# Experts taken in an order that is listed on the chip, and computed in 64-row parts first

## The chip, the cores and the metric

The kernel runs on one NeuronCore of a Trainium2 chip. The metric is device time in microseconds (us) of one execution, the median of several runs. The kernel before takes 1252.5 us (three runs: 1251.7, 1252.5, 1255.65).

The engines are named as in the profile: PE (TensorE, matrix multiplication; PEld are its weight loads), DVE (VectorE), ACT (ScalarE), POOL (GpSimd) and SP (SyncE, which here only issues DMAs). Each engine works through its own queue in order and waits for the others by semaphores.

## The reference, cut to what matters

One layer of a streaming encoder on 512 tokens of 1024 features. A token mixer (projection, gated MLP, gated delta rule, output projection) comes first; then a layer norm; then a hierarchical mixture of experts, which is what the change touches; then a last layer norm.

```python
def _hier_moe(x, w_rg, b_rg, w_re, b_re, w1, w3, w2):
    pg = softmax(xt @ w_rg + b_rg); grp = argmax(pg)            # top 1 of 4 groups
    le = (xt @ w_re + b_re) of that group                        # 8 experts in a group
    top_v, top_i = lax.top_k(le, MOE_TOPK)                       # top 2 of the 8
    gate = p_grp * softmax(top_v)
    eid = grp * MOE_EXPERTS_PER_GROUP + top_i                    # 32 experts
    ...
    hb = silu(xb @ w1[e]) * (xb @ w3[e]);  y = hb @ w2[e]        # 1024 -> 512 -> 1024
    ...
    out = sum over the two experts of gate * y
```

The 1024 pairs (512 tokens, two experts each) are spread unevenly. The reference's routing of the inputs that the kernel gets, experts 0 to 31 in four groups of eight:

```
all tokens       1   0   2   2   1   2   1   1
                57  55  40  18  94  83  37 130
                34  22  82 104  15  18 126  19
                 0  11   8   5  26  15  13   2
first 256        0   0   1   2   1   1   1   0
                29  30  16  11  40  36  16  62
                18  12  43  54   5  12  65   5
                 0   7   5   4  17   8  11   0
```

Two experts (1 and 24) get no token; five (0, 1, 7, 24, 31) get none from the first 256 tokens. Eleven get more than 32, six more than 64, three more than 96, none more than 160.

## The kernel before, in words

The program has a front (normalisation, projections, gated MLP, delta rule, merge), which the change leaves alone. Then come three stages.

**Output projection, first norm, router** (`out_ln1`, `Router`). The 512 tokens are four tiles t of 128. For each tile PE does 48 matmuls (`po`, helper line L416), transposes the rows (`ph`, L433) and multiplies them with the router's weights (`lps`, L987). DVE makes the tile's logits (`lg`, L991), and `Router.tile` finds the two experts of each token (`ek`, L1078), marks them (`mk`, `M`), counts with small matmuls how many earlier tokens chose the same expert (`cps`, L1083), and scatters the token's number into its expert's list (`sps`, L1097). After the last tile `sort` writes the lists of token rows, `idx`: up to 160 (NB) per expert. The instruction order of this stage is set by a scheduler from its own estimates.

**The experts** (`Experts.run`), written by hand in order. A block b is one expert: position b in the list `blocks`, which goes through j = 0 to 7 and within it through the groups, so experts 0, 8, 16, 24, 1, 9, 17, 25, 2 and so on. An expert's weights are six chunks of 1 MB: four of w1 and w3 together (chunks 0 to 3), two of w2 (4, 5). SP loads them in the order in which PE uses them: chunks 0 to 3 of block b, then 4 and 5 of block b-1. There are 18 buffers (`raws`), used in turn; a load waits until the matmuls that read its buffer's chunk of 18 places earlier are done, and until the load eight places earlier has landed. The first 18 loads are unconditional (13 go out early, the last five, `late`, once the router's memory is free); each later one has a condition on its expert's count and moves nothing for an empty expert.

In step b the program does: gather the rows of block b+2 from DRAM (`fetch`, POOL; 64 rows, and 96 more if the count is over 64); `up` of block b on PE (x times w1 and w3); silu and product (`gate`: ACT, DVE); `turn_x` of block b+1 (PE transposes, DVE scales the result into `x`); `down` of block b-1 on PE (h times w2); `turn` of block b (PE transposes h, ACT copies); `store_y` of block b-1 (DVE and ACT copy out of PSUM, POOL issues the stores to `y_dram`). `up` and `down` work in parts (`parts`): rows 0 to 31 always (the small part: 32-column weights, four column groups of PE side by side), rows 32 to 95 if the count is over 32, rows 96 to 159 if it is over 96 (the large parts: 64 columns, two groups). Up to five copies of a block for counts over 160 follow in a loop; here it runs zero times.

**The end** (`finish_rows`, `finish`): SP loads the normalised rows and the gain and bias rows behind the last weights, ACT and DVE scale them, then, after the loop's barrier, POOL gathers each token's two expert rows from `y_dram`, and DVE, ACT and POOL do the last norm.

In the profile L1371 is `up`'s matmul, L1399 `down`'s, L1350 and L1356 the transposes of `turn_x`, L1385 and L1387 those of `turn`, L1378 and L1379 `gate`, L1407 and L1410 the copies of `store_y`, L1416 its stores, L1331 the gathers, L396 and L398 the weight loads without and with a condition, L1248 and L1283 the clearing before the first block. Line numbers of the changed kernel differ: there L417 is `po`, L1127 `cps`, L1141 `sps`, L397 and L399 the loads, L1484 and L1489 the stores.

## Time and profile before

| | us |
|---|---|
| median of three runs | 1252.5 |
| the profiled execution | 1258.0 |
| its span, first to last instruction | 1256.0 |
| before the first expert's matmul | 703.0 |
| from there to the end of the last | 495.4 |
| after it | 57.6 |

One execution was profiled; its span is 2 us shorter than its time, and its time is 5.5 us over the median. Times of instructions are counted from the span's start. In the span cut into 40 slices (31.4 us each) a digit is the busy share in tenths; "GB/s" is what the DMA engines moved. TensorE's mean granted clock over the span is 0.937. A matmul of 32-bit floats shows as two records. Of the DMAs, 192 weight loads are issued, and those whose condition is false move nothing.

### The profile page before, as it was taken

The page shows a single profiled execution, that of the slowest core. Times are in us where ns is not written, and L with a number is a line of the kernel's source. Part 1 is how long each engine was busy: PE and PEld are TensorE (multiplying, and loading weights), DVE is VectorE, ACT ScalarE, POOL GpSimd, SP SyncE. Part 2 cuts the span into 40 slices and gives each one's busy share as a digit, 9 for nine tenths or more (in the row PEclk, how much of TensorE's full clock was granted, in tenths as well). Part 3 has the DMA queues.
Part 4 walks back from the last instruction along what each step waited for, and adds up shares of the span by engine and source line. Part 5 has one row for each costly group of instructions (what it writes and reads, how often), then busy time and mean ns, then how long its engine had stood idle before and what let it go on. Part 6 is the DMA issues. An engine that isn't in the chain of part 4 may idle for free. (4 is left out here: it accounts for less than half of the span.)

```text
span 1256.0 us, 20781 instructions
## 1 busy us (share of the span) xinstructions
PE 1080.5 (86%) x7740; PEld 708.2 (56%) x7740; DVE 616.5 (49%) x1266; ACT 440.0 (35%) x902; POOL 185.6 (15%) x374
## 2 busy tenths in 40 slices
PE   4999999999999999999999688898798786799910
PEld 2888788867777777667887344444344333234400
DVE  7566444567667777744754434423123132222256
ACT  6333355444545455435331222323122222122221
POOL 1000100311321133300000111112011111011034
PEclk9999999999999999999999799999799798799965
DMA  4422533899112122015674749999999999999953
GB/s 171 151 84 68 164 90 121 288 339 356 56 63 68 35 67 68 24 45 189 218 284 165 267 161 397 408 398 403 407 400 406 400 414 410 385 418 386 405 188 129
DMA packets 77182, 298.15 MB, mean 237 GB/s; under 512 B 9360, under 2 KB 34208, under 8 KB 53248
## 3 DMA queue, kind: packets, MB, share of 16 engines
q1 hardware_dynamic: 66960, 274.22, 57.9%
q0 software_dynamic: 7504, 17.20, 4.1%
q10 hardware_dynamic: 2592, 4.99, 1.1%
q8 instruction: 86, 1.41, 0.5%
q14 instruction: 40, 0.33, 0.1%
HBM read 277.36 MB, written 50.35 MB: 261 GB/s over the span
## 5 line engine op out<-in xcount | busy, mean ns | idle before, releaser
L1371 PE MATMUL u<-raw,x 128*32 128x256 f32 (+1 forms) x2496 | 231.5, 440 | 30.1 <-DMA raw<-in_w 27.7
L213 PE MATMUL psi<-hTh,lo 128*128 128x512 f32 x448 | 183.7, 412 | 1.6 <-DVE lo L213 1.6
L213 PE MATMUL psi<-hTh,hi 128*128 128x512 f32 x448 | 184.0, 414 | 0.9 <-ACT hi L213 0.5
L213 PE MATMUL psi<-hTl,hi 128*128 128x512 f32 x448 | 183.6, 412 | 0.0
L1371 PEld LDWEIGHTS u<-raw,x 128*32 128x32 f32 (+1 forms) x2496 | 96.8, 119 | 150.2 <-issue 69.1
L1379 DVE TENSOR_TENSOR h<-h,u 128x640 f32<-128x640 f32 x32 | 26.3, 821 | 307.1 <-ACT h L1378 307.1
L213 DVE TENSOR_TENSOR lo<-raw,hi 128x1024 fp32r<-128x1024 f32 x74 | 91.4, 1236 | 78.5 <-ACT hi L213 77.5
L213 ACT CAST hi<-raw 128x1024 fp32r<-128x1024 f32 x74 | 77.5, 1047 | 120.2 <-PE psi L213 103.2
L1399 PE MATMUL yz<-raw,hT 128*32 128x256 f32 x1024 | 80.6, 457 | 21.3 <-DMA raw<-in_w 10.3
L213 PEld LDWEIGHTS psi<-hTh,lo 128*128 128x128 f32 x448 | 84.8, 189 | 21.4 <-issue 3.9
L213 PEld LDWEIGHTS psi<-hTh,hi 128*128 128x128 f32 x448 | 85.0, 190 | 20.5 <-issue 2.8
L213 PEld LDWEIGHTS psi<-hTl,hi 128*128 128x128 f32 x448 | 84.8, 190 | 17.3 <-issue 1.6
L1378 ACT ACTIVATE h<-u 128x640 f32<-128x640 f32 x32 | 22.5, 703 | 178.7 <-PEq L1319 130.6
L1410 ACT COPY ylarge<-y 64x512 f32<-64x512 f32 x128 | 74.3, 580 | 9.1 <-DMA y_dram<-ylarge 7.6
L1407 DVE COPY ysmall<-yz 32x256 f32<-32x256 f32 x128 | 53.5, 418 | 44.5 <-PE yz L1399 36.5
L1388 ACT COPY hT<-t 128x128 f32<-128x128 f32 x32 | 8.5, 265 | 190.7 <-PE t L1385 190.7
L1399 PEld LDWEIGHTS yz<-raw,hT 128*32 128x32 f32 x1024 | 39.0, 126 | 49.3 <-issue 25.9
L1416 POOL DMA_DIRECT2D y_dram<-ysmall x32 | 15.9, 497 | 304.7 <-DVE ysmall L1407 267.5
L213 DVE SCALAR_TENSOR_TENSOR acc<-xp,cols,acc 128x512 f32<-128x512 f32 x72 | 54.6, 759 | 4.7 <-ACT acc L213 3.5
L1399 PE MATMUL y<-raw,hT 128*64 128x512 f32 x224 | 51.0, 602 | 0.0
L1350 PE MATMUL t<-ident,mh 64*128 64x64 f32 x256 | 24.5, 240 | 23.3 <-PEq L1319 14.8
L1350 PEld LDWEIGHTS t<-ident,mh 64*128 64x128 f32 x256 | 20.4, 151 | 42.8 <-issue 39.8
(403 smaller groups left out, 1764.9 us busy)
## 6 DMA issues: line engine op xcount, KB each, us to landing
raw<-in_w SPq DMA_DIRECT2D x192, 1024.0 KB, 20.7
raw<-in_wt SPq DMA_DIRECT2D x73, 512.0 KB, 3.8
y_dram<-zero SPq DMA_DIRECT2D x48, 512.0 KB, 6.5
y_dram<-ylarge POOLq DMA_DIRECT2D x128, 128.0 KB
raw<-in_wv SPq DMA_DIRECT2D x8, 512.0 KB, 7.6
raw<-in_wo SPq DMA_DIRECT2D x4, 1024.0 KB, 8.2
y_dram<-ysmall POOLq DMA_DIRECT2D x32, 128.0 KB
vt<-in_x SPq DMA_DIRECT2D x4, 512.0 KB
```

The costliest lines, as they stand in the source:

```text
L213: op._ins = getattr(getattr(self.nc, op.attr), op.name)(*map(real, op.args), **{k: real(x) for k, x in op.kw.items()})
L1350: nc.tensor.transpose(self.t[0][:, k * NA:k * NA + NA], r[0][:, k * 128:k * 128 + 128], ident[0:NA, 0:NA])
L1371: self.nc.tensor.matmul(self.u[q * r:(q + 1) * r, NP if p is None else p, 0:c], x[:, k, r0:r0 + r], self.raw[b, k // 2][:, o:o + c], start ...
L1378: self.nc.scalar.activation(out=h, in_=u[:, :, 0], func=AF.Silu)
L1379: self.nc.vector.tensor_mul(out=h, in0=h, in1=u[:, :, 1])
L1388: self.nc.scalar.copy(out=x[:, n], in_=self.t[1][:, 0:128])
L1399: self.nc.tensor.matmul(y[q * r:(q + 1) * r, 0:c], t[:, i, j * r:(j + 1) * r], self.raw[b, 4 + k // 2][:, o:o + c], start=k == 0, stop=k == 3)
L1407: nc.vector.tensor_copy(out=small[:, q], in_=self.y0[q * 32:(q + 1) * 32, 0:256])
L1410: nc.scalar.copy(out=large[:, q, p], in_=self.y[p][q * 64:(q + 1) * 64])
L1416: nc.gpsimd.dma_start(out=dst.rearrange("r (q n) -> r q n", q=src.shape[1]), in_=src, cond=c > 32 * j)
```

## The change

**The order of the experts.** `Router.order` runs between tiles 1 and 2. It counts, for the first 256 tokens, how many chose each expert, flags the experts with at least one (the first three of the old order, 0, 8 and 16, are always flagged), and writes a list `ord` of 32 places: the flagged experts in the old order, but the last four of them at the very end, and the unflagged ones just ahead of these four. With these inputs the list is 0, 8, 16, 9, 17, 25, 2, 10, 18, 26, 3, 11, 19, 27, 4, 12, 20, 28, 5, 13, 21, 29, 6, 14, then 24, 1, 7, 31, then 22, 30, 15, 23. Marking, counting and scattering (`place`) work with places in this list instead of experts, and so have to follow it: those of tiles 0 and 1 both come after `order`. Blocks 0 to 2 load their weights by fixed addresses; from block 3 on SP loads the expert's number (`ordi`) into a register and the weights from an address made with it.

**The parts.** Large parts of 64 rows come first: rows 0 to 63 if the count is over 32, rows 64 to 127 if it is over 96. What is left over, if anything, is the small part of 32 rows, which starts at row 0, 64 or 128. `units` makes three numbers per expert: the count (at most 160), the rest d behind the large parts, and the small part's first row r0. The small part, always done before, is done only if d is over 0; so a count of 0, of 33 to 64 or of 97 to 128 has none. Its 32 columns stand in a tile of their own, `xs`, which DVE fills first, and for counts over 64 fills again from the row r0.

**The stores.** The small part is stored at a row made with r0, if d is over 0. A large part is stored in two DMAs of 64 rows by 512 columns, where it was two of 32 rows by 1024. ACT's four copies of 64 partitions are two of 128.

**Clearing.** PSUM is cleared by six ACT copies with scale 0 instead of DVE, the unused columns of `x` by POOL.

The diff, without the changes of the overflow loop and of constants:

```diff
@@ -38,6 +38,7 @@
+NPRE = 3
...
@@ -990,6 +991,11 @@
                 router.tile(t)
+                if t == 1:
+                    router.order()
+                    router.place(0)
+                if t:
+                    router.place(t)
...
+
+    def order(self):
+
+
+        nc, W, cst, v, g = self.nc, self.W, self.cst, self.nc.vector, self.nc.gpsimd
+        for t in range(2):
+            q = W.tile([128, 2, E], BF, name="oq")
+            v.tensor_tensor(out=q, in0=bc(cst["iota"][:, 0:E], 2, 1), in1=bc(self.ek[:, :, t], E, 2), op=OP.is_equal)
+            for k in range(2):
+                nc.tensor.matmul(self.cps[:, NT], cst["ones_bf"], q[:, k], start=t + k == 0, stop=t + k == 2)
+        f = W.tile([128, E], F32, name="of_")
+        v.tensor_scalar(f.rearrange("p (j g) -> p j g", g=4), self.cps[:, NT].rearrange("p (g j) -> p j g", g=4),
+                        0.0, None, op0=OP.is_gt)
+        v.memset(f[:, 0:NPRE], 1.0)
+        r = W.tile([128, E], F32, name="or_")
+        v.tensor_tensor_scan(r, cst["ones"][:, 0:E], f, 0.0, OP.mult, OP.add)
+        b = W.tile([128, 2], F32, name="ob_")
+        v.tensor_scalar(b[:, 0:1], r[:, E - 1:E], -4.0, float(NPRE), op0=OP.add, op1=OP.max)
+        v.tensor_scalar(b[:, 1:2], r[:, E - 1:E], -1.0, float(E), op0=OP.mult, op1=OP.add)
...
+        eq = W.tile([128, E, E], F32, name="oeq")
+        v.tensor_tensor(out=eq, in0=bc(p0, E, 1), in1=bc(cst["iota"][:, 0:E], E, 2), op=OP.is_equal)
+        g.tensor_tensor(out=eq, in0=eq, in1=bc(cst["seq"], E, 1), op=OP.mult)
+        v.tensor_reduce(out=self.ord, in_=eq, axis=AX.X, op=OP.add)
+        v.tensor_copy(out=self.ordi, in_=self.ord)
+
+    def place(self, t):
+
+        nc, W, cst, v = self.nc, self.W, self.cst, self.nc.vector
         mk = self.mk[:, :, t]
-        v.tensor_tensor(out=mk, in0=bc(cst["iota"][:, 0:E], 2, 1), in1=bc(ef, E, 2), op=OP.is_equal)
+        v.tensor_tensor(out=mk, in0=bc(self.ord, 2, 1), in1=bc(self.ek[:, :, t], E, 2), op=OP.is_equal)
         v.tensor_tensor(out=self.M[:, t], in0=mk[:, 0], in1=mk[:, 1], op=OP.add)
...
+    def units(self, W, n, out):
+
+
+        v, w = self.nc.vector, n.shape[1]
+        a = W.tile([128, 3, w], F32, name="un%d" % w)
+        v.tensor_scalar(a[:, 1], n, 32.0, 64.0, op0=OP.is_gt, op1=OP.mult)
+        v.tensor_scalar(a[:, 2], n, 96.0, 64.0, op0=OP.is_gt, op1=OP.mult)
+        v.tensor_tensor(out=a[:, 2], in0=a[:, 2], in1=a[:, 1], op=OP.add)
+        v.tensor_scalar(a[:, 0], n, float(NB), None, op0=OP.min)
+        v.tensor_tensor(out=a[:, 1], in0=a[:, 0], in1=a[:, 2], op=OP.subtract)
+        v.tensor_copy(out=out, in_=a)
+
...
     def clear(self):
 
-        for t in [self.u[:, 0:NP]] + self.y + [x[:, :, NA:96] for x in self.x]:
-            self.nc.vector.memset(t, 0.0)
+        for t in [self.u[:, NP, 0:256]] + [self.u[:, p] for p in range(NP)] + [self.y0[:, 0:256]] + self.y:
+            n = t.shape[1] // 128
+            self.nc.scalar.activation(out=t.rearrange("p (a n) -> p a n", a=n), in_=bc(self.cst["ident"], n, 1),
+                                      func=AF.Copy, scale=0.0)
 
...
         load(len(kk.raws) - late, True)
+        if clear:
+            for x in self.x:
+                nc.gpsimd.memset(x[:, :, NA:96], 0.0)
         for b in range(min(2, nb)):
             self.fetch(b, 0)
+        if clear:
+            clear()
         next(more, None)
         for b in range(min(2, nb)):
             self.fetch(b, 1)
         if clear:
-            clear()
 
...
     def parts(self, b, f):
 
-        n = self.n(b)
-        f(b, None)
+        n, d = self.n(b), self.n(b, ET.PE, 1)
+        with self.tc.If(d > 0):
+            f(b, None)
         with ExitStack() as st:
             for p in range(NP):
                 st.enter_context(self.tc.If(n > 32 + 64 * p))
...
-        affine(slice(0, NA), ((self.t[0], 0, KD),))
+        affine(xs, slice(0, 32), ((self.t[0], 0, KD),))
+        affine(x, slice(0, NA), ((self.t[0], 0, KD),))
...
         with self.tc.If(self.n(b, ET.DVE) > NA):
-            affine(slice(NA, NB), zs)
+            affine(x, slice(NA, NB), zs)
+            v.tensor_copy(out=xs, in_=x[:, :, ds(self.n(b, ET.DVE, 2), 32)])
 
     def place(self, p):
 
-        return (4, 0, 32) if p is None else (2, 32 + 64 * p, 64)
+        return (4, 0, 32) if p is None else (2, 64 * p, 64)
...
-        x, (n, r0, r) = self.s[b]["x"], self.place(p)
+        x, (n, r0, r) = self.xs[b % 2] if p is None else self.s[b]["x"], self.place(p)
...
@@ -1402,22 +1475,19 @@
     def store_y(self, b):
         nc, row = self.nc, self.blocks[b][0]
         small = self.yp.tile([32, 4, 256], F32, name="ysmall")
-        large = self.yp.tile([64, 2, NP, 512], F32, name="ylarge")
+        large = self.yp.tile([128, NP, 512], F32, name="ylarge")
         for q in range(4):
             nc.vector.tensor_copy(out=small[:, q], in_=self.y0[q * 32:(q + 1) * 32, 0:256])
         for p in range(NP):
+            nc.scalar.copy(out=large[:, p], in_=self.y[p])
+        n, d, r0 = (self.n(b, ET.Pool, i) for i in range(3))
+        nc.gpsimd.dma_start(out=self.y_dram[ds(row + r0, 32), :], in_=small.rearrange("r q n -> r (q n)"), cond=d > 0)
+        for p in range(NP):
+            r = row + 64 * p
+            dst = self.y_dram[r:r + 64, :] if isinstance(row, int) else self.y_dram[ds(r, 64), :]
             for q in range(2):
-                nc.scalar.copy(out=large[:, q, p], in_=self.y[p][q * 64:(q + 1) * 64])
-        c = self.n(b, ET.Pool)
-
-        def store(j, src):
-            r = row + j * 32
-            dst = self.y_dram[r:r + 32, :] if isinstance(row, int) else self.y_dram[ds(r, 32), :]
-            nc.gpsimd.dma_start(out=dst.rearrange("r (q n) -> r q n", q=src.shape[1]), in_=src, cond=c > 32 * j)
-
-        store(0, small)
-        for j in range(2 * NP):
-            store(1 + j, large[j % 2 * 32:j % 2 * 32 + 32, :, j // 2])
+                nc.gpsimd.dma_start(out=dst[:, q * 512:(q + 1) * 512], in_=large[q * 64:(q + 1) * 64, p],
+                                    cond=n > 32 + 64 * p)
...
@@ -1574,9 +1644,9 @@
 
 
 
-    blocks = [(e * NB, static(e), r.idx[0:NA, 0, e:e + 1], r.idx[0:NB - NA, 1, e:e + 1], r.cnti[0:1, e:e + 1],
-               True)
-              for i, e in enumerate(g * 8 + j for j in range(8) for g in range(4))]
+    blocks = [(e * NB, static(e % 4 * 8 + e // 4) if e < NPRE else dynamic(r.ordi[0:1, e:e + 1]), r.idx[0:NA, 0, e:e + 1],
+               r.idx[0:NB - NA, 1, e:e + 1], [r.cnti[0:1, i, e:e + 1] for i in range(3)], e >= NPRE)
+              for e in range(E)]
     with tc.manual_schedule():
         ex.run(blocks, rest, ex.clear)
         for _ in rest:
...
```

In the next three places the rows are those of one engine's queue, in order; x4 is a row four times over.

PE in `out_ln1`, around the last matmuls of tile 2 and the first of tile 3 (`po`; its weight tiles are hi and lo, `mh` and `ml` the tokens). Before:

```order
L416 MATMUL po<-lo_4855,mh 128x512 x4
L416 MATMUL po<-hi_4839,mh 128x512
L416 MATMUL po<-hi_4839,ml 128x512
L416 MATMUL po<-hi_4839,mh 128x512
L416 MATMUL po<-hi_4839,ml 128x512
L433 MATMUL ph<-ident,h1s_4469 128x128 [waits DVE_49]
```

With the change:

```order
L417 MATMUL po<-lo_4857,mh 128x512 x3
L1127 LDWEIGHTS ustrict
L1127 MATMUL cps<-M,ustrict 128x32 [waits DVE_49]
L417 MATMUL po<-lo_4857,mh 128x512
L417 MATMUL po<-hi_4841,mh 128x512
L1127 LDWEIGHTS ones_bf
L1127 MATMUL cps<-M,ones_bf 128x32 [waits DVE_49]
```

The counting matmuls of tiles 0 and 1, which stood in their own tiles, now stand before tile 2's last matmul and wait there for DVE's `M`, which waits for the list.

POOL in `store_y` of one block (DMASW_n are the lanes on which its DMAs report; ISA rows set the condition). Before:

```order
L1416 DMA y_dram<-ysmall 32x1024 [waits DMASW5_49,DVE_49]
L1416 ISA
L1416 DMA y_dram<-ylarge 64x1x512 [waits DMASW6_49,Activation_49]
```

With the change:

```order
L1379 TENSOR_LOAD cnti x2
L1484 ISA
L1484 DMA y_dram<-ysmall 32x1024 [waits DMASW7_49,DVE_49]
L1489 ISA
L1489 DMA y_dram<-ylarge 64x512 [waits DMASW7_49,DMASW0_49,Activation_49]
```

POOL reads d and r0 into registers at this place, and the first large store now also waits for the lane of the small store ahead of it (DMASW7), that is, until that has landed.

SP at the first expert's loads (DMAHW_n: lanes of SP's DMAs), from the change:

```order
L397 DMA raw_5396<-in_w 128x2048 [waits DMAHW0_49,DVE_49,PE_49]
L1639 TENSOR_LOAD ordi [waits DVE_49]
L397 ISA
L397 DMA raw_5397<-in_w 128x2048 [waits DMAHW1_49,DVE_49,PE_49]
```

The load of an expert's number stands ahead of its first chunk; before, the row ahead of a DMA without condition was the DMA of the chunk before it.

More of the change, by code (lines that the diff above doesn't have):

```diff
@@ L1078, in tile @@
         v.tensor_copy(out=ef, in_=e8[:, 0:2])
+    def order(self):
[14 more added lines that the diff above has]
+        v.tensor_scalar(b[:, 1:2], r[:, E - 1:E], -1.0, float(E), op0=OP.mult, op1=OP.add)
+        p0 = W.tile([128, E], F32, name="op0")
+        v.scalar_tensor_tensor(out=p0, in0=cst["iota"][:, 0:E], scalar=b[:, 0:1], in1=r, op0=OP.add, op1=OP.subtract)
+        p1 = W.tile([128, E], F32, name="op1")
+        v.tensor_scalar(p1, r, b[:, 0:1], b[:, 1:2], op0=OP.is_gt, op1=OP.mult)
+        v.scalar_tensor_tensor(out=p1, in0=r, scalar=-1.0, in1=p1, op0=OP.add, op1=OP.add)
+        v.tensor_tensor(out=p1, in0=p1, in1=p0, op=OP.subtract)
+        v.tensor_tensor(out=p1, in0=p1, in1=f, op=OP.mult)
+        v.tensor_tensor(out=p0, in0=p0, in1=p1, op=OP.add)
+        eq = W.tile([128, E, E], F32, name="oeq")
[3 more added lines that the diff above has]
+        v.tensor_copy(out=self.ordi, in_=self.ord)
@@ L1119, in rest @@
         yield
-        v.tensor_copy(out=self.cnti, in_=cnt)
+        self.units(R, cnt, self.cnti)
         gs = R.tile([128, NT, 4], F32, name="gs")
@@ L1165, in rest @@
         ot = R.tile([128, 7, NX * E], F32, name="ot")
-        for j, src in enumerate((cst["eidx"], stb[:, 0].rearrange("p b e -> p (b e)"),
+        ei = R.tile([128, NX, E], F32, name="ei")
+        v.tensor_copy(out=ei, in_=bc(self.ord, NX, 1))
+        for j, src in enumerate((ei.rearrange("p b e -> p (b e)"), stb[:, 0].rearrange("p b e -> p (b e)"),
                                  stb[:, 1].rearrange("p b e -> p (b e)"))):
@@ L1170, in rest @@
             v.tensor_reduce(out=self.of[:, j], in_=ot, axis=AX.X, op=OP.add)
-            if j < 2:
-                v.tensor_copy(out=self.oi[:, j], in_=self.of[:, j])
+            if j == 0:
+                v.tensor_copy(out=self.oi[:, 0], in_=self.of[:, 0])
             yield
+        self.units(R, self.of[:, 1], self.oi[:, 1:4])
+        yield
         dst = R.tile([128, NT, E], F32, name="dst")
@@ L1240, in __init__ @@
         self.x = [xt.tile([128, KD, NB], F32, name="x%d" % i) for i in range(2)]
+        self.xs = [xt.tile([128, KD, 32], F32, name="xs%d" % i) for i in range(2)]
         self.hp = self.ec(self.tile_pool(name="ehp", bufs=1))
@@ L1306, in run, with n @@
             next(more, None)
-    def n(self, b, e=ET.PE):
+    def n(self, b, e=ET.PE, i=0):
         s = self.s[b]
-        if ("n", e) not in s:
-            s["n", e] = self.nc.values_load(self.blocks[b][4], engines=(e,), min_val=-T, max_val=T,
-                                            skip_runtime_bounds_check_because="counts of tokens")
-        return s["n", e]
+        if ("n", e, i) not in s:
+            lo, hi = ((0, NB), (-64, 32), (0, 128))[i]
+            s["n", e, i] = self.nc.values_load(self.blocks[b][4][i], engines=(e,), min_val=lo, max_val=hi,
+                                               skip_runtime_bounds_check_because="counts of tokens")
+        return s["n", e, i]
     def parts(self, b, f):
-        n = self.n(b)
-        f(b, None)
+        n, d = self.n(b), self.n(b, ET.PE, 1)
+        with self.tc.If(d > 0):
+            f(b, None)
         with ExitStack() as st:
```

28 lines of the change are left out of this document (16 added, 12 removed).

## The prediction

> **What bounds the kernel now.** I read the page first, then the slices, stage windows, SP's timeline and PE's timeline at the experts' end. PE looks like the bound (86% busy), but the slices say otherwise for the second half.
>
> ```profile
> PE   4999999999999999999999688898798786799910
> DMA  4422533899112122015674749999999999999953
> GB/s 171 151 84 68 164 90 121 288 339 356 56 63 68 35 67 68 24 45 189 218 284 165 267 161 397 408 398 403 407 400 406 400 414 410 385 418 386 405 188 129
> ```
>
> From slice 25 to 38 the DMA engines are full at about 400 GB/s. The windows give the edges of that stretch.
>
> ```profile
> 700.00:722.00 22.00, 17.64 (x173) 8.82 (x175) 5.83 (x24) 1.55 (x3) 1.99 (x3) 0.79 0.93 351
> 722.00:741.00 19.00, 17.25 (x170) 7.80 (x170) 6.72 (x13) 4.47 (x8) 1.67 (x6) 1.00 0.08 17
> 741.00:1195.00 454.00, 379.05 (x3839) 177.24 (x3832) 129.90 (x248) 109.68 (x203) 61.21 (x178) 0.91 1.01 402
> 1195.00:1256.00 61.00, 2.43 (x37) 1.38 (x35) 37.39 (x49) 12.35 (x16) 22.44 (x25) 0.55 0.42 151
> ```
>
> The last two columns are DMA share and GB/s. For 454 us the DMA is the bound (1.01); just before, for 19 us, it does nearly nothing (0.08) while 182 MB (454 us at 402 GB/s) are still to come. SP's rows say why.
>
> ```profile
> 700.84 2.91 SPq L396 DMA_DIRECT2D raw<-in_w  x5
> 708.07 20.03 SPq L398 DMA_DIRECT2D raw<-in_w  x10
> 739.12 2.49 SPq L398 DMA_DIRECT2D raw<-in_w  x4
> raw<-in_w SPq DMA_DIRECT2D x192, 1024.0 KB, 20.7
> q1 hardware_dynamic: 66960, 274.22, 57.9%
> q0 software_dynamic: 7504, 17.20, 4.1%
> ```
>
> Blocks 3 and 4 are experts 24 and 1, which are empty. Of the ten loads issued from 708.07, only block 2's two w2 chunks move anything: the other eight places in the list are the empty experts' (chunks 2 and 3 of block 3, all of block 4, 4 and 5 of block 3). The next real load needs `up` of block 2 to end, and goes out at 739.12. So the empty experts use up buffers when PE has none to give back. Ten of the 192 loads move nothing; two of the empty experts' twelve are among the 18 unconditional ones.
>
> **The change, term by term**, against the profiled span of 1256.0. A chunk is 1.049 MB, so at 402 GB/s 2.61 us. Landing 20.7 us after issue means that eight share the engines.
>
> *The gap.* With the new list, what follows `up` of block 0 is block 3's and 2's chunks and then block 4's, all real: four at about 708, six more after `up` of block 1. Backlog at 708 is still the five late loads (13 us), so the gap goes: 0.92 x 19 = **-17.5**.
>
> *Two chunks fewer.* The empty experts now stand at places 24 and 25, where all twelve loads have a condition: 2 x 2.61 = **-5.2**.
>
> *The list.* It lengthens the router's chain.
>
> ```profile
> 665.24 0.17 DVE L1078 CAST ek<-e 128x2 f32<-128x2 uint32 x1
> 665.94 0.18 PE L1083 MATMUL cps<-M,ustrict 128*128 128x32 bf16 x1 [0.35 <-DVE M L1081]
> 674.74 0.39 PE L416 MATMUL po<-hi,mh 128*128 128x512 f32 x1
> 727.38 0.86 DVE L1155 TENSOR_TENSOR ov<-inc,iota 128x672 f32<-128x672 f32 x1 [0.22 <-DVEq L1357]
> 754.98 0.85 DVE L1170 TENSOR_REDUCE of<-ot 128x7 f32<-128x672 f32 x1
> L1033 POOL TENSOR_TENSOR raw<-raw,raw 128x1024 f32<-128x1024 f32 x3 | 7.0, 2337 | 6.7 <-DVE ve L369 5.8 <-DVE nm L373 0.9
> 689.83 0.69 DVE L977 SCALAR_TENSOR_TENSOR h1s<-po,h1s 128x512 f32<-128x512 f32 x1 [5.96 <-PE po L416]
> 690.55 0.69 DVE L979 BATCH_NORM_STATS2 st<-h1s 128x6 f32<-128x512 f32 x1
> ```
>
> From `ek` of tile 1 (665.4): some 13 small DVE steps at about 0.23 apart (3.0), tile 2's addition and statistics that stand between them (1.4), the comparison and the sum over 1024 elements (0.86 and 0.85 for 672, so 1.3 each), POOL's product (2.34), the marks (1.0): 10.3, so `M` at about 675.7. PE reaches the waiting matmul, one before tile 3's at 674.74, at about 673.9 (six matmuls moved away ahead of it): a stall of 1.8. The ones moved here add 1.2 more, and all that follows on PE and DVE, up to the last tile's list, is later by **3** (bounds 0 and 6: the stall vanishes, or doubles). The late loads wait for DVE's clearing:
>
> ```profile
> 698.16 0.91 DVE L1248 MEMSET u<- 128x1024 f32 x1 [0.21 <-issue]
> 699.13 1.03 DVE L1248 MEMSET y<- 128x512 f32 x2
> 700.20 0.55 DVE L1248 MEMSET x<- 128x256 f32 x2
> ```
>
> These 2.5 go to ACT and POOL, and six small steps (`units`, 1.3) come: 1.2 back. The stream starts **+1.8** later. ACT's six copies end before `up` of block 0 needs them, since its x must first be gathered; if not, PE starts 1 or 2 us later, which the stream doesn't feel.
>
> *A hole at the empties.* Places 24 and 25 use twelve of 18 buffers. After the chunks of block 23 and 22 that are eight in flight, the next real one (block 26) needs `up` of block 23 done. Eight that share the engines have some 4.5 chunks of work left together; when the fourth lands, 1.25 (3.3 us). `up` ends 1.7 after it, and a load needs some 2 us before it moves anything (estimate from the 256 KB stores' 2.0 to landing, below). I take **+2** (0 to 6).
>
> ```profile
> h_dram<-h1s ACTq DMA_DIRECT2D x8, 256.0 KB, 2.0
> L1416 POOL DMA_DIRECT2D y_dram<-ysmall x32 | 15.9, 497 | 304.7 <-DVE ysmall L1407 267.5 <-DVE stb L1163 21.1 <-DMA y_dram<-ysmall 16.1
> ```
>
> *Stores in pieces of 2 KB.* The rows stored stay the same. The 14 large parts' 3.67 MB cost at q0's 51.5 us per 17.2 MB 11.0. By bytes halving the pieces is free, by packets it adds 11. q1's mean packet is 4.1 KB at 2.65 us per MB, q0's 2.3 KB at 2.99: nearly half the size, 13% dearer. So **+2**.
>
> *PE.* Nine small parts go (37 to 57, 104, 126 tokens and the empties), some 5.6 us of PE each, and each `parts` gets a branch and each block a register load, below 0.5. In a stretch where PE waits for weights neither shows.
>
> *The tail.* Where PE follows the last weights, the order of the last experts counts.
>
> ```profile
> 1152.09 18.29 PE L1371 MATMUL u<-raw,x 128*32 128x256 f32 x128
> 1178.11 0.68 PE L1350 MATMUL t<-ident,mh 64*128 64x64 f32 x8 [0.34 <-PEq L1319]
> 1179.09 1.93 PE L1399 MATMUL yz<-raw,hT 128*32 128x256 f32 x32 [0.30 <-PEq L1353]
> 1180.95 7.09 PE L1399 MATMUL y<-raw,hT 128*64 128x512 f32 x32
> 1188.66 3.66 PE L1371 MATMUL u<-raw,x 128*32 128x256 f32 x64
> 1196.46 1.93 PE L1399 MATMUL yz<-raw,hT 128*32 128x256 f32 x32 [0.96 <-ACT hT L1389]
> ```
>
> Before, expert 15 (130 tokens: 18.3 us of `up`, 9.0 of `down`) is third from last, and 16 chunks follow its w13 (42 us), in which PE catches up: it ends at 1198.4, 3.4 after the stream (1195). Now expert 15 is the last but one, and ten chunks follow (26.1). From its last w13 chunk on PE does: rest of the small part 0.9, both large parts and branches 14.2, `turn_x` 1.6, `down` of expert 30 2.3, `turn` 0.7, `up` of 23 4.0, `turn_x` place 1.6, `down` of 15 9.3, `turn` and ACT's copies 2.0, `down` of 23 1.9: 38.5. So PE ends 12.4 after the stream: **+9** (5 to 14).
>
> [...]
>
> *The end.* ACT's L1410 copies halve, but the stores of 130 tokens now precede the last ones by one block, and the first of them waits for the small one: I take it over as it was, 57.6.
>
> Sum: -17.5 - 5.2 + 1.8 + 2 + 2 + 9 = -7.9, a span of 1248.1; the median stands 3.5 under the span: **1244.5**.
>
> **The rivals.**
>
> *PE does not lag at the end.* Then the tail's 9, and perhaps the hole and the pieces (4), fall away: 1231.5 to 1235.5. For it: the stream was the bound up to 1195 and PE 0.83 busy. Against: the chain above is made of quoted matmuls. 0.2.
>
> *The gain is given back in the stores.* If a 2 KB piece costs like a 4 KB one, +9, and if the large store's wait for the small one holds ACT's queue in the tail (the next silu is behind its copies), some 2 more: 1253.5 to 1256. For it: smaller packets are dearer by the byte. Against: q0's are dearer by 13% only, at nearly half q1's size. 0.15.
>
> *SP becomes the bound: slower.* 162 moving loads get an address from a register, which no row here shows. Now four loads take SP 2.49, 0.62 each. From 2.61 per load on SP sets the pace and every 0.1 us costs 16: at 2.8, 31 us, so 1276. Against: the loads with a condition use a register too and are no dearer than those without (2.91 for five). 0.12.
>
> That the list misses the empties is excluded by the table of the first 256 tokens: experts 1 and 24 are unflagged.
>
> **How the numbers follow.** Forecast 0.53. Less than 0.3% (3.8 us) can't be told from no change. Of the forecast's own spread (1238 to 1251, by the start, the hole and the tail) 0.48 lies below 1248.7; with the first rival that is 0.68 faster. The rest, 0.05 of the forecast and most of the stores, is 0.19 same; SP and the stores' far end 0.13 slower. Range: all bounds good and half the tail, 1232; hole, start and tail bad, 1257.
>
> **What would show it.** DMA share near 1 from 701 on without the 19 us at 0.08; last weight at about 1178; expert 15's `up` starting some 26 us before that and PE ending 12 after; an idle DMA of a few us around 1065; the last tile's `h1s` about 3 later than 689.83 (quoted). It is wrong if SP's loads come more than 2.61 apart with fewer than eight in flight, if chunks take over 2.7 in the full stretch, or if PE ends within 5 us of the last landing.

## The result, and the profile after

The changed kernel takes 1245.92 us (median of five runs, 1242.91 to 1248.74), the kernel before 1255.65 in the same comparison: a ratio of 0.9926, with a 95% interval of 0.9897 to 0.9955. Measured a second time, beside the first experiments, it was 0.9902 (0.9880 to 0.9925). The forecast was 1244.5 in a range of 1232 to 1257, so it holds. Whether its steps hold is another matter, and the experiments found some that don't.

The slices of the changed kernel, as they were shown of the one before (31.0 us each):

```profile
DMA  4422433899222121113673799999999999999942
GB/s 172 156 83 69 156 99 105 284 347 358 76 69 53 50 69 52 35 52 135 244 303 106 285 371 406 396 410 401 417 392 415 397 412 400 381 384 386 387 121 109
```

Its windows: the two that held the old gap, the full stretch, the place of the empty experts, and the tail from expert 22 on (columns: length, busy time of the five engines, granted clock, DMA share, GB/s).

```profile
700.00:722.00 22.00, 12.21 (x101) 6.43 (x103) 6.19 (x17) 2.08 (x5) 1.86 (x2) 0.70 1.00 361
722.00:741.00 19.00, 15.88 (x108) 6.85 (x106) 8.43 (x17) 3.23 (x6) 0.73 (x5) 1.00 0.93 372
741.00:1176.00 435.00, 334.26 (x3079) 154.41 (x3077) 153.91 (x318) 73.89 (x145) 61.68 (x177) 0.89 1.01 401
1060.00:1068.00 8.00, 2.76 (x29) 1.74 (x25) 4.85 (x10) 2.53 (x5) 0.66 (x4) 0.81 0.75 288
1109.40:1184.00 74.60, 69.11 (x564) 29.66 (x564) 19.44 (x39) 10.33 (x21) 8.23 (x25) 0.96 0.93 366
```

The 19 us that stood at a DMA share of 0.08 are now at 0.93. At the empties there is a hole of 8 x 0.25 = 2 us. The rate in the full stretch is the same, 401 GB/s. Now the end of the stream and the tail, on SP and PE; the last of SP's `in_rows` loads goes out as the last weight lands, eight loads behind it, so the end of its group marks the landing. Before:

```profile
1187.45 8.31 SPq L1009 DMA_DIRECT2D raw<-in_rows  x4
```

With the change:

```profile
1161.76 7.84 SPq L1015 DMA_DIRECT2D raw<-in_rows  x4
1146.27 3.66 PE L1444 MATMUL u<-raw,xs 128*32 128x256 f32 x64
1149.86 13.96 PE L1444 MATMUL u<-raw,x 128*64 128x512 f32 x64
1174.33 7.09 PE L1472 MATMUL y<-raw,hT 128*64 128x512 f32 x32
1182.08 1.93 PE L1472 MATMUL yz<-raw,hT 128*32 128x256 f32 x32
```

The last weight lands at 1169.6 instead of 1195.8, and PE, with expert 15's `up` and `down` in the tail, ends at 1184.0, 14.4 behind it; before it was 2.6. So 12 of the 26 us by which the last weight lands earlier are given back in the tail, about as forecast.

All kernels of this study in the same stages, each from its one profiled run. "h1s" is the start of DVE's last `h1s`, which ends the router's input; "late" the first of the five late loads, "landed" the last weight. The time up to h1s differs by a few us between profiled runs of one kernel (687.5 and 689.3 for the changed one), so it is left out here.

| kernel | h1s to late | late to landed | to PE's end | to the end | ratio to before |
|---|---|---|---|---|---|
| before | 11.0 | 494.9 | 2.6 | 57.6 | 1 |
| changed | 9.2 | 472.9 | 14.4 | 57.2 | 0.9926 |
| changed, again | 9.2 | 476.1 | 13.5 | 57.6 | 0.9902 |
| old list | 9.2 | 499.8 | 5.8 | 61.1 | 1.0055 |
| order alone | 11.0 | 470.3 | 21.2 | 58.7 | 0.9968 |
| empties early | 9.2 | 495.5 | 8.1 | 59.3 | 1.0056 |
| small part always | 9.2 | 485.1 | 20.6 | 57.7 | 1.0047 |
| clearing on DVE | 13.2 | 469.9 | 13.5 | 57.8 | 0.9927 |
| list fixed | 9.6 | 475.0 | 12.8 | 57.3 | 0.9892 |
| reversed | 9.2 | 477.0 | 5.4 | 60.0 | 0.9908 |
| light last | 9.2 | 478.8 | 0.7 | 61.9 | 0.9876 |
| light last, large stores first | 9.2 | 477.4 | 2.2 | 55.1 | 0.9866 |
| rows early | 9.2 | 476.7 | 12.9 | 57.9 | 0.9907 |
| order alone, light last | 11.1 | 471.2 | 1.8 | 55.7 | 0.9794 |

The ratios' intervals are about 0.002 to either side (0.0014 for the order alone, 0.003 for the first measurement of the changed kernel). One thousandth is 1.26 us.

### The profile page after: what moved, and what is told of

Its sections match the earlier page's. It is cut to its first block, busy times and chain, and to the rows that moved or that the text cites. A ratio compares the mean times of both kernels' runs of the same rounds, so it can differ in the third digit from the quotient of the medians.

```text
span 1241.2 us, 19396 instructions
## 1 busy us (share of the span) xinstructions
PE 1031.0 (83%) x6880; PEld 681.0 (55%) x6880; DVE 645.1 (52%) x1358; ACT 403.3 (32%) x844; POOL 192.0 (15%) x377
## 3 DMA queue, kind: packets, MB, share of 16 engines
q1 hardware_dynamic: 66672, 272.13, 57.9%
q0 software_dynamic: 7504, 17.20, 4.3%
## 5 line engine op out<-in xcount | busy, mean ns | idle before, releaser
L1444 PE MATMUL u<-raw,xs 128*32 128x256 f32 x1472 | 100.1, 421 | 31.0 <-DMA raw<-in_w 27.8
L1444 PE MATMUL u<-raw,x 128*64 128x512 f32 x448 | 105.0, 623 | 6.6 <-PEq L1386 2.7
L214 PEld LDWEIGHTS psi<-hTh,lo 128*128 128x128 f32 x448 | 84.5, 189 | 21.2 <-issue 3.9
L1444 PEld LDWEIGHTS u<-raw,xs 128*32 128x32 f32 x1472 | 48.4, 118 | 74.6 <-DMA raw<-in_w 35.1
L1444 PEld LDWEIGHTS u<-raw,x 128*64 128x64 f32 x448 | 34.4, 144 | 71.6 <-issue 59.2
L1472 PE MATMUL y<-raw,hT 128*64 128x512 f32 x224 | 60.2, 692 | 15.4 <-PEq L1386 12.7
L1472 PE MATMUL yz<-raw,hT 128*32 128x256 f32 x736 | 52.3, 420 | 12.6 <-PEq L1425 6.1
L1489 POOL DMA_DIRECT2D y_dram<-ylarge x128 | 19.5, 154 | 195.4 <-DMA y_dram<-ysmall 115.3
L1421 PE MATMUL t<-ident,mh 64*128 64x64 f32 x256 | 23.7, 238 | 27.2 <-PEq L1388 15.9
L1472 PEld LDWEIGHTS y<-raw,hT 128*64 128x64 f32 x224 | 19.4, 158 | 48.9 <-issue 48.6
```

Of the source, the lines that this page charges most:

```text
L214: op._ins = getattr(getattr(self.nc, op.attr), op.name)(*map(real, op.args), **{k: real(x) for k, x in op.kw.items()})
L1421: nc.tensor.transpose(self.t[0][:, k * NA:k * NA + NA], r[0][:, k * 128:k * 128 + 128], ident[0:NA, 0:NA])
L1444: self.nc.tensor.matmul(self.u[q * r:(q + 1) * r, NP if p is None else p, 0:c], x[:, k, r0:r0 + r], self.raw[b, k // 2][:, o:o + c], start ...
L1472: self.nc.tensor.matmul(y[q * r:(q + 1) * r, 0:c], t[:, i, j * r:(j + 1) * r], self.raw[b, 4 + k // 2][:, o:o + c], start=k == 0, stop=k == 3)
L1489: nc.gpsimd.dma_start(out=dst[:, q * 512:(q + 1) * 512], in_=large[q * 64:(q + 1) * 64, p], cond=n > 32 + 64 * p)
```

## The experiments

The theory is the prediction's: the loads are the bound, the list takes the gap out of them, and the heavy expert near the end gives half of it back. The chief rival: it is the time that the 64-row parts save PE.

**The changed kernel again, and with the old list.** The second is made by flagging every expert, so that the list, computed as before, comes out as the old order.

```diff
-        v.memset(f[:, 0:NPRE], 1.0)
+        v.memset(f, 1.0)
```

> The changed kernel once more, as the yardstick of this call. Both theories: the ratio to the kernel before is 0.993 as measured (0.990 to 0.9955).

> Every expert is flagged, so that the computed list is the old order; parts, stores, clearing and the list's own cost stay. Theory (the order is what counts, the loads are the bound): against the changed kernel the gap comes back (DMA idle 18.6 us of the first 40 before, 3.3 now: +15), two more chunks are loaded (2.1 MB at 2.5 us: +5), and PE ends 3 us after the last landing as it did before, not 14.4 (-11.5): +9 in all, ratio to before about 1.000. Rival (the gain comes from the parts: PE busy 334 of 435 us in the full stretch against 379 of 454): the gain stays, ratio 0.993 or less.

Measured: 0.9902 and 1.0055. The rival is out: with the parts but without the order the kernel is slower than before. But the distance is 19 us where the theory gave 9. Some 6 of these ten stand behind the last landing: PE ends 5.8 behind it, not 3, and the end is 61.1, not 57.6. The others stand in the gap. The first 45 us from the first late load on, old list:

```profile
698.60:743.60 45.00, 29.52 (x202) 13.89 (x202) 13.31 (x34) 8.54 (x16) 4.39 (x9) 0.74 0.49 176
```

Before:

```profile
700.80:745.80 45.00, 39.26 (x377) 17.96 (x375) 15.60 (x39) 6.03 (x11) 4.07 (x9) 0.91 0.60 224
```

A DMA share of 0.49 against 0.60: the gap is 23 us with the changed parts, clearing and stores, and was 18. PE has done less by then (29.5 us of work against 39.3). POOL's first gather and PE's first matmuls say what is late. Before:

```profile
697.75 1.12 POOL L1331 DMA_INDIRECT mh<-h_dram,idx  x1 [5.36 <-DVE idx L1103]
700.37 1.09 PE L1350 MATMUL t<-ident,mh 64*128 64x64 f32 x8 [2.85 <-DMA mh<-h_dram,idx]
702.97 4.94 PE L1371 MATMUL u<-raw,x 128*32 128x256 f32 x64 [1.51 <-DVE x L1347]
```

With the change:

```profile
687.49 0.69 DVE L978 SCALAR_TENSOR_TENSOR h1s<-po,h1s 128x512 f32<-128x512 f32 x1 [5.95 <-PE po L417]
696.41 1.13 POOL L1400 DMA_INDIRECT mh<-h_dram,idx  x1 [0.85 <-DVE cnti L1257]
696.71 3.14 SPq L397 DMA_DIRECT2D raw<-in_w  x5
703.38 1.09 PE L1421 MATMUL t<-ident,mh 64*128 64x64 f32 x8 [8.19 <-DMA mh<-h_dram,idx]
707.02 5.06 PE L1444 MATMUL u<-raw,xs 128*32 128x256 f32 x64 [2.56 <-DVEq L1429]
```

From the gather's start to PE's first transpose it was 2.6 us and is now 7.0 (+4.4): the five late loads (5 MB) go out 0.3 us behind it, where they went out 3.1 behind it before. The gather starts 1.0 later against h1s, with the `units` ahead of it (its wait names `cnti`), and from the transposes to `up` it is 1.0 more, with four DVE operations for `x` in place of two. So PE's first `up` starts 19.5 us after h1s; it was 13.1. Loads wait for PE's `up` there, so the stream feels it.

**The order alone.** The kernel before with the changed kernel's list in its program text.

```diff
-              for i, e in enumerate(g * 8 + j for j in range(8) for g in range(4))]
+              for i, e in enumerate((0, 8, 16, 9, 17, 25, 2, 10, 18, 26, 3, 11, 19, 27, 4, 12, 20, 28, 5, 13, 21,
+                                     29, 6, 14, 24, 1, 7, 31, 22, 30, 15, 23))]
```

> The kernel before with nothing but the order: its list of experts, in the program text, is the one that the changed kernel makes on the chip (0, 8, 16, 9, 17, 25, ..., 24, 1, 7, 31, 22, 30, 15, 23). Parts, stores, clearing, marks and fixed addresses as before. Theory (the order brings the stream's gain, the 64-row parts matter only where PE does not wait, which is at the front and from expert 22 on): loads start 11 after h1s, PE 13; the gap goes (-15 to -18) and two chunks (-5); but expert 22 (126 tokens) has its small part again in the tail, so PE ends 18 to 21 after the last landing (+15 to +18), as with the small part always done: -4 to -8 in all, ratio 0.994 to 0.997. Rival (the parts are worth nothing in this order, and the order is all): 0.990 or less.

Measured: 0.9968, as the theory said. Stage by stage the stream is 24.6 shorter (20 to 23 were expected), and PE ends 21.2 behind it. Its first 45 us, then those of the changed kernel's two profiles:

```profile
699.20:744.20 45.00, 39.23 (x376) 17.93 (x375) 15.60 (x39) 6.04 (x11) 4.08 (x9) 0.91 1.00 387
696.70:741.70 45.00, 28.80 (x210) 13.60 (x212) 15.79 (x38) 8.57 (x16) 4.39 (x9) 0.82 0.94 355
698.50:743.50 45.00, 29.38 (x202) 13.80 (x202) 13.76 (x34) 8.56 (x16) 4.21 (x5) 0.75 0.88 335
```

With the order alone the DMAs are never idle there. In the changed kernel the share was 0.94 and 0.88, so its own front loses 3 to 5 us that the order had won. What its parts win is in the tail, 21.2 to 14: expert 22 (126 tokens) has no small part any more.

**The empties early.** The place of the unflagged experts is one constant of the list.

```diff
-        v.tensor_scalar(b[:, 0:1], r[:, E - 1:E], -4.0, float(NPRE), op0=OP.add, op1=OP.max)
+        v.tensor_scalar(b[:, 0:1], r[:, E - 1:E], -24.0, float(NPRE), op0=OP.add, op1=OP.max)
```

> The unflagged experts (24, 1, 7, 31) stand ahead of the last 24 flagged ones instead of the last four, so at places 4 to 7; experts 24 and 1 at 4 and 5, with all loads conditional; the tail (22, 30, 15, 23) stays. Theory: the twelve loads that move nothing use up buffers while PE has none to give back: 15 to 20 us of DMA idle between 715 and 750, the hole of 2 us near 1063 gone, PE still some 14 after the last landing: +13 to +18 against the changed kernel, ratio 1.004 to 1.007. Rival (the gap came from the loads' conditions or from the first blocks' size, not from the empties' place): no change, 0.993.

Measured: 1.0056, 19 us slower than the changed kernel. The first 60 us:

```profile
699.90:759.90 60.00, 41.32 (x263) 18.69 (x263) 20.11 (x50) 11.04 (x21) 7.53 (x16) 0.81 0.60 214
```

24 us idle, of which the changed kernel has 3 to 5 in its own first 60. All loads of the empty experts have a condition here, so it is their place and not the missing condition that made the gap. The same twelve skipped loads cost some 20 us at places 4 and 5 and 2 us at 24 and 25.

One thing came out otherwise than expected: PE ends 8.1 behind the last landing, not some 14, though the last four experts are the same. There PE still waits for expert 15's last chunk of w1 and w3, and needs 35.2 us from then to its end (1203.5):

```profile
1168.31 1.07 PE L1444 MATMUL u<-raw,xs 128*32 128x256 f32 x16 [1.21 <-DMA raw<-in_w]
```

In the changed kernel PE waits for no weight over 0.5 us from expert 22 on. The four unflagged experts stand just ahead of it there: from the end of the `up` before them (expert 14's, 1056.8) to the start of expert 22's (1109.4) PE takes 53 us, and then it finds the weights there. That their steps hold up PE is read from these rows; that the tail is 5 to 6 us shorter with them elsewhere is what the run shows.

**The small part always done.** The branch around the small part is removed; stores stay conditional.

```diff
-        with self.tc.If(d > 0):
-            f(b, None)
+        f(b, None)
```

> The small part is computed for every expert, needed or not (its rows are stored only where needed, as in the changed kernel): nine more small parts of 5.6 us on PE, 50 us in all. Theory (the loads bound the stretch, PE has 100 us of slack in it): all of it is hidden except that of expert 22 (126 tokens), which stands where PE no longer waits: +4 to +7 against the changed kernel, ratio 0.994 to 0.996, by a PE end some 19 after the last landing. Rival (the time saved on PE is what made the kernel faster): +20 to +50.

Measured: 1.0047, 18 us over the changed kernel: neither. The tail does what the theory said (PE ends 20.6 behind, +7). But the stream is 9 to 12 us longer, and it loses 4 to 6 of them at the front:

```profile
696.30:741.30 45.00, 30.79 (x298) 15.37 (x300) 13.05 (x33) 7.86 (x15) 4.21 (x5) 0.74 0.80 298
```

On PE's timeline, block 1's large part:

```profile
724.49 7.09 PE L1443 MATMUL u<-raw,x 128*64 128x512 f32 x32
```

In the changed kernel:

```profile
717.38 8.44 PE L1444 MATMUL u<-raw,x 128*64 128x512 f32 x32 [0.52 <-PEq L1386]
```

Blocks 1 and 2 (57 and 34 tokens) have their small parts back, and the large part starts 7 us later. Between 1060 and 1100, behind the empty experts' place, the DMA share is 0.89 where it was 0.96 and 0.95, some 2 to 3 us more; the rest of the 9 to 12 was not found. The other six small parts, some 34 us of PE work, are hidden but for these, as forecast. So the parts count above all in two places: at the front, where they pay for the late start of PE, and behind expert 22.

**The clearing on DVE again**, ahead of the late loads' release, as before.

```diff
-        for t in [self.u[:, NP, 0:256]] + [self.u[:, p] for p in range(NP)] + [self.y0[:, 0:256]] + self.y:
-            n = t.shape[1] // 128
-            self.nc.scalar.activation(..., func=AF.Copy, scale=0.0)
+        for t in [self.u[:, NP, 0:256], self.u[:, 0:NP], self.y0[:, 0:256]] + self.y + [x[:, :, NA:96] for x in self.x]:
+            self.nc.vector.memset(t, 0.0)
...
         if clear:
-
+            clear()
             for i in range(late):
```

> The clearing of PSUM and of x goes back to DVE, ahead of its release of the five late weight loads; all else as changed. Theory (the first gather is late because the late loads now go out with it: it took 5.8 us from its end of issue to PE's first transpose against 1.5 before, so PE's first up starts 19.5 us after the last tile's h1s against 13.1, and the DMA idles 2 to 5 us more between 15 and 35 us into the stream): the loads start some 3 us later (12 after h1s, not 9.2), the gather lands before them, PE's first up starts at about 14 to 15 after h1s, and that idle time goes; net -2 to +1.5 against the changed kernel. Rival (the start of the loads sets everything behind it): +3.

Measured: 0.9927 (0.9905 to 0.9950). Times cannot tell it from the changed kernel, but its trace shows the mechanism:

```profile
699.10 1.13 POOL L1393 DMA_INDIRECT mh<-h_dram,idx  x1 [5.93 <-DVE idx L1147]
701.61 1.08 PE L1414 MATMUL t<-ident,mh 64*128 64x64 f32 x8 [2.75 <-DMA mh<-h_dram,idx]
703.81 3.14 SPq L397 DMA_DIRECT2D raw<-in_w  x5
```

And its first 45 us from the late loads on:

```profile
703.80:748.80 45.00, 34.25 (x231) 14.88 (x233) 18.71 (x48) 6.62 (x13) 4.25 (x13) 0.89 0.99 387
```

The loads go out 4.0 later, the gather is back at 2.5 us, PE's first `up` starts 16.1 after h1s, and the DMAs don't idle any more; the stream is 3 to 6 shorter. What the earlier loads won, the gather and the idle time had taken.

**The list fixed in the program**, with fixed addresses, and the marks placed tile by tile as before: no counting, no loads by register.

```diff
-                if t == 1:
-                    router.order()
-                    router.place(0)
-                if t:
-                    router.place(t)
+                router.place(t)
...
-    blocks = [(e * NB, static(e % 4 * 8 + e // 4) if e < NPRE else dynamic(r.ordi[0:1, e:e + 1]), ...
+    blocks = [(e * NB, static(LIST[e]), ...
```

> The changed kernel with its list fixed: the router's table is set by POOL early, the marks are placed tile by tile as before, the weights have fixed addresses, and no list is counted. Theory (a load by register costs SP 0.73 us against 0.62, far below 2.6, and the list's chain cost 1.05 us: from the first tile's ek to the last tile's h1s 40.75 against 39.71): -1 against the changed kernel, ratio 0.989, the stream unchanged (473 to 477). Rival (SP's register loads and the list hold up the stream): the stream shorter by 5 or more.

Measured: 0.9892, 1.3 us under the changed kernel, the stream 475.0. So the list and the loads by register cost about 1 us together, which is less than the interval of 2.5 us to either side: SP is no bound.

**Other ends of the list.** Two base orders that keep expert 15 out of the last four; in the second the unflagged experts also stand ahead of twelve instead of four.

```diff
-        iota("seq", [128, E], [[1, 8], [8, 4]], 0, 0)
+        (seq made of pieces: j = 0, 7, 6, 5, 4, 3, 2, 1; or j = 0, 2, 3, 4, 5, 6, 7, 1)
-        v.tensor_tensor(out=q, in0=bc(cst["iota"][:, 0:E], 2, 1), ...
+        v.tensor_tensor(out=q, in0=bc(cst["seq"], 2, 1), ...
...
-        v.tensor_scalar(b[:, 0:1], r[:, E - 1:E], -4.0, float(NPRE), op0=OP.add, op1=OP.max)
+        v.tensor_scalar(b[:, 0:1], r[:, E - 1:E], -12.0, float(NPRE), op0=OP.add, op1=OP.max)
```

The last line's change is the second order's alone.

> The base order goes through j = 0, 7, 6, 5, 4, 3, 2, 1 (seq, and the flags counted in its order); so the list is 0, 8, 16, 15, 23, 6, 14, 22, 30, ... 18, 24, 7, 31, 1, 26, 9, 17, 25: the heavy expert 15 is at place 3, the last four have 8, 55, 22 and 11 tokens. Theory: stream as it is (169.6 to 1173 at its end, empties apart so no hole, perhaps 2 to 5 us lost early since 15, 14 and 22 hold buffers), PE 3 to 4 after the last landing in place of 14.4: -6 to -11 against the changed kernel, ratio 0.984 to 0.988. Rival (the finish, not the expert's weight, sets the distance between the last landing and the end; or heavy experts early starve the loads): no gain, 0.993 or more.

> Base order j = 0, 2, 3, 4, 5, 6, 7, 1, and the unflagged experts ahead of the last twelve flagged ones: 0, 8, 16, 2, 10, ..., 28, 5, then 24, 7, 31, 1, then 13, 21, 29, 6, 14, 22, 30, 15, 23, 9, 17, 25; the last four have 19, 55, 22 and 11 tokens, and the heavy ones stand neither first nor just ahead of the empty ones. Theory: no new hole, stream as changed (473 to 476), PE ends 3 to 5 after the last landing, not 14 (-9 to -10), and the end is 2 to 3 longer, since the rows loaded behind the last weights land 10 us after them, as in the reversed list (60.0 against 57.4): -6 to -8, ratio 0.984 to 0.986. Rival (what PE lags is covered by the loads and the scaling of the end anyway, so the order of the last experts is worth nothing): 0.990.

Measured: 0.9908 and 0.9876. PE's distance from the last landing falls as expected, to 5.4 and 0.7. The first gains nothing by it, the second 3 us where 6 to 8 were expected. In both the end is longer, 60.0 and 61.9. In the first that is not all: its stream is 1 to 4 us longer, and its h1s comes at 691.1. The light-last run's timeline shows the end's chain on POOL and DVE:

```profile
1175.86 0.51 POOL L1486 DMA_DIRECT2D y_dram<-ysmall  x1 [6.26 <-DVE ysmall L1482]
1182.18 1.71 DVE L1482 COPY ysmall<-yz 32x256 f32<-32x256 f32 x4 [6.61 <-DMA y_dram<-ysmall]
1185.19 0.49 POOL L1486 DMA_DIRECT2D y_dram<-ysmall  x1 [1.59 <-issue]
1190.40 0.04 POOL L1491 DMA_DIRECT2D y_dram<-ylarge  x1 [4.71 <-DMA y_dram<-ylarge]
```

A small store of 128 KB took 6 us to land while the rows behind the weights (4 MB) came in (issued at 1175.86 to 1176.37, and DVE goes on at 1182.18); DVE's next copy into the single buffer waits for it, then POOL's stores for the next landing. With PE 14 behind, those rows come in earlier: in the changed kernel POOL goes on 2.4 us after the issue of its last small store (1187.44 to 1189.86, 1.92 of them waiting, at a DMA share of 0.26).

**Large stores first**, with the light-last list: the small store behind the large ones, two buffers for its rows, and a constant (`eidnb`) folded into two operations to make room.

```diff
+        self.ysp = self.ec(self.tile_pool(name="eysp", bufs=2))
-        nc.gpsimd.dma_start(out=self.y_dram[ds(row + r0, 32), :], ..., cond=d > 0)
         for p in range(NP):
             ...
+        nc.gpsimd.dma_start(out=self.y_dram[ds(row + r0, 32), :], ..., cond=d > 0)
```

> The light-last list, computed on the chip, and in each block's stores the large ones ahead of the small one, with two buffers for the small part's rows: so DVE's last copies no longer wait 6.6 us for the landing of the small store before, and POOL's last stores no longer for it either; now a small store waits for the large ones of its own block. (The constant eidnb is folded into two operations to make room for the buffer.) Theory (the last small store's landing sets the barrier: issued 7 us after PE's end in the light-last run, landed at 12.1, first gather at 18.9): it goes out 3 to 4 earlier, -2 to -4 against the light-last run (0.9876), ratio 0.985. Rival (the landing of the rows behind the last weights and their scaling set the barrier anyway): 0.9876.

Measured: 0.9866, against 0.9876 not told apart. By stages the end is 6.8 us shorter, more than expected. The last copies and stores, and the end's first gather:

```profile
1185.34 1.71 DVE L1482 COPY ysmall<-yz 32x256 f32<-32x256 f32 x4 [3.80 <-PE yz L1474]
1188.46 0.50 POOL L1492 DMA_DIRECT2D y_dram<-ysmall  x1 [1.00 <-issue]
1195.46 1.47 POOL L1030 DMA_INDIRECT raw<-y_dram,yi  x1 [6.51 <-issue]
```

DVE now waits for PE, and the first gather of the end comes 10.2 after PE's end instead of 18.0. But h1s came at 696.5, 6 us later than in the light-last run (690.4), and PE was busy 75.3 of the first 100 us instead of 81.9. The edit takes an instruction out of the front, whose order a scheduler sets. That this costs the 6 us is a guess: the thirteen other profiles have PE busy 81.1 to 82.0 there, but no run changes this alone.

**The rows scaled early**, on the changed kernel's list.

```diff
+            if b == nb and end:
+                end()
             if b:
                 self.parts(b - 1, self.down)
...
```

Here `end` issues the loads of the rows, ACT's two copies and four of DVE's eight operations; the other four follow the last stores.

> The list as changed; the scaling of the normalised rows (two ACT copies and the first four of DVE's eight operations) is issued ahead of the last expert's down instead of behind its stores, the other four right behind them and ahead of the barrier. Theory: the rows land at about 8 after the last weight, ahead of PE's end; now ACT reaches them only 6 us after PE's end, and five of DVE's operations run beside POOL's first gathers, which then take 1.9 us each to issue against 1.0; so the end shrinks from 57.4 to 51 to 54: -3 to -6 against the changed kernel. Rival (the last store's landing and the barrier set the end): 0 to -1.

Measured: 0.9907, nothing won; half of the theory held. POOL's gathers of the end, first in the changed kernel, then here:

```profile
1196.72 1.90 POOL L1028 DMA_INDIRECT raw<-y_dram,yi  x1 [5.57 <-issue]
1198.92 1.94 POOL L1028 DMA_INDIRECT raw<-y_dram,yi  x1 [0.30 <-issue]
```

```profile
1205.26 1.06 POOL L1030 DMA_INDIRECT raw<-y_dram,yi  x1 [5.57 <-issue]
1206.62 1.03 POOL L1030 DMA_INDIRECT raw<-y_dram,yi  x1 [0.30 <-issue]
```

From the first gather to the end it is 40.9 instead of 44.5. But the gather itself starts 16.9 after PE's end instead of 12.7: ACT had the copies of `turn` and a large store ahead of the rows, so DVE's four operations began at 1189 and held up its last copies.

**The order alone, light experts last**: the kernel before with the light-last list in its text (edit as for the order alone).

> The kernel before with the list of the run with the light experts last (0, 8, 16, 2, 10, ..., 5, 24, 7, 31, 1, 13, ..., 15, 23, 9, 17, 25) in the program text, all else as before. Theory: the gap and two chunks go as above (-20 to -23), and PE ends 1 to 5 after the last landing, since no heavy expert is among the last four; the end is 58 to 62: -17 to -22, ratio 0.983 to 0.987, as fast as the changed kernel with that list (0.9876) or faster, since the parts have little left to hide. Rival (without the 64-row parts PE does not keep up with the loads): 0.992 or more.

Measured: 0.9794 (0.9774 to 0.9814), 1231.3 us: the fastest of all, 14 us under the changed kernel and 4 us under the least that was expected (0.983 to 0.987). The end is 55.7, where 58 to 62 was expected. Its whole stream has no idle place:

```profile
697.40:742.40 45.00, 38.83 (x384) 17.88 (x382) 15.59 (x39) 6.29 (x12) 4.07 (x9) 0.94 1.00 390
742.40:1168.60 426.20, 360.14 (x3798) 168.61 (x3801) 127.20 (x240) 110.46 (x205) 60.54 (x177) 0.95 1.01 403
```

PE does 360 us of work in these 426 (334 of 435 in the changed kernel) and still ends 1.8 after the last landing. Its list fits these inputs and would have to be made on the chip for others, which by the fixed-list run costs about 1 us.

The two lists and the old one, with old and with changed parts, stores and clearing:

| list | old parts | changed parts |
|---|---|---|
| old | 1 | 1.0055 |
| the change's | 0.9968 | 0.9902 (0.9926) |
| light last | 0.9794 | 0.9876 |

The rest of the change (parts, stores, clearing and the making of the list) costs 7 us with the old list, brings 5 to 8 with its own, and costs 10 with a list whose tail is light.

## Why the prediction was right, and where not

The sum came out nearly as forecast, -7.9 against -9 to -12, but in part by luck, through errors that cancelled. By its steps:

- **The bound and the gap** (-17.5): right. The first 45 us idle 2.7 or 5.4 us (shares 0.94, 0.88) where it was 18: -13 to -15. The rest is lost to the new late start of PE: with the order alone the idle time is gone entirely. The empties' place as the cause is shown by the early-empties run.
- **Two chunks fewer** (-5.2): right. The page's two DMA queues:

```profile
q1 hardware_dynamic: 66672, 272.13, 57.9%
q0 software_dynamic: 7504, 17.20, 4.3%
```

q1 moves 2.09 MB less than before, 5.2 us at 402 GB/s.
- **The list** (chain +3, start +1.8): too dear, and wrong in sign. From the first tile's `ek` to the last h1s it is 40.75 instead of 39.71, so +1.0; from h1s to the late loads it is 1.8 less: the start is 0.8 earlier.
- **"If not, PE starts 1 or 2 us later, which the stream doesn't feel"**: wrong, and the first of the steps that failed. PE starts 6.4 later against h1s, 4.4 of it because the earlier loads crowd the first gather (the clearing on DVE brings these back). The stream loses 3 to 6 us (order alone and clearing on DVE against the changed kernel).
- **The hole** (+2): right, 2.0.
- **Pieces of 2 KB** (+2): the worry was empty. In the kernel before, too, a row of a large part lay in its buffer in two pieces of 2 KB (`ylarge` was [64, 2, NP, 512]), so nothing was halved there. Packets and bytes are the same, 7504 and 17.20 MB. q0's time, its share times the span, is 50.9 to 53.4 us in the profiles with the changed stores and 51.5 to 52.5 in those with the old ones: no difference shows.
- **PE's parts** ("neither shows"): wrong too. PE does not wait for weights everywhere: done always, the small parts cost 18 us, 9 to 12 in the stream (4 to 6 at its front) and 7 in the tail.
- **The tail** (+9, with 12.4 behind the last landing): right in kind and near in size, 13.5 and 14.4, but partly by luck. The sum starts at the landing of expert 15's last chunk of w1 and w3 and takes 38.5 us from there. In the early-empties run, where PE does wait for that chunk, it is 35.2. In the changed kernel PE doesn't wait for it: it is already nearly without pause from expert 22 on (69.1 of 74.6 us busy in the last window above) and comes to expert 15 late. PE also loses clock there, behind waits of 1.4 and 2.1 us:

```profile
1109.44 15.54 PE L1444 MATMUL u<-raw,x 128*64 128x512 f32 x64 [1.44 <-ACT ylarge L1482]
1137.18 8.46 PE L1472 MATMUL y<-raw,hT 128*64 128x512 f32 x32 [2.08 <-PEq L1386]
```

These are expert 22's; the same matmuls of expert 15 take 13.96 and 7.09, at a granted clock of 1.00. For expert 22 it is 0.71 from 1109.4 to 1115.0 and 0.66 from 1135 to 1140, so 1.6 and 1.4 us are lost, 3.0 together, for which the sum has no term. They make PE later at expert 15. In the changed kernel's other windows above the clock is 0.70 where PE is busy 12.2 of 22 us, 0.89 at 334 of 435 and 1.00 at 15.9 of 19, but 0.81 at 2.8 of 8; no run tries apart what lowers it.
- **The end** (unchanged): right in sum, 57.2 and 57.6, by two opposite changes: three of DVE's eight operations on the rows run ahead of the barrier where six did. So the first gather comes 12.7 after PE's end instead of 16.0, and 44.5 us instead of 41.6 follow it, since five of the operations now stand behind the barrier, beside POOL's gathers.

With the stream 18.8 to 22.0 shorter (forecast 18.7), the tail 10.9 to 11.8 longer (9) and the start 0.8 earlier (1.8 later), the stages give -9 to -11. The stream's terms as measured (-13 to -15, -5.2 and +2) come to -16 to -18 only: about 3 us of its gain have no term.

The rivals: **PE does not lag** is out by the rows of the tail. **The stores** are out here (the end is not longer), but the wait that they were to bring, the large store's for the small one, and DVE's for its buffer, is real: it shows where the tail is light, and with the large stores first the end is 6.8 us shorter there. **SP as the bound** is out: fixed addresses and a fixed list together bring about 1 us.

## What to carry to other kernels

Where one transfer stream is the bound, a list of work items is judged at three places: where the consumer has not yet freed buffers (empty items there stopped the stream for some 20 us), where the empties stand (just ahead of heavy items they left PE behind, and the tail was 5 to 6 us shorter with them elsewhere), and behind the last transfer (what is heavy there is paid for: 12 of the 26 us won went there). Saved compute was worth something here mostly at the ends of the stream, so the same edit can gain with one order and lose with another: try each part of a change with the order it will run in. And a transfer released earlier can be paid back by the small one beside it that the critical engine is waiting for: the first gather reached PE 4.4 us later here.

## What the runs showed of the hardware that was not expected

- A gather of 64 rows (256 KB) that starts the pipeline took 2.5 to 2.6 us to reach PE alone and 7.0 with 5 MB of loads issued 0.3 us behind it; a 128 KB store took 6 us to land while other loads came in (the light-last run).
- POOL took 0.99 to 1.06 us to issue a gather with DVE idle (the first three of the rows-early run), and 1.90 to 1.94 while DVE multiplied or added two operands (the changed kernel's first three). But the changed kernel's last two, both beside such operations, took 0.99 and 2.04, and the light-last run's first, beside another, 1.05. So the rows agree in direction only, and what links the two was not tried apart.
